# Softmax over 16384 rows: chunks of 17 and 15 rows per partition instead of 16

## Chip, cores, metric

One core of a Trainium2 chip. The metric is the device time of one execution in microseconds (us), lower is better. All runs quoted here were in the fast state. A profile is one execution; its span is 1.8 to 1.9 us shorter than the time measured for it.

## The reference

```python
batch, seq, dim = 16, 1024, 512            # x: float32, random normal
x_max = np.max(x, axis=-1, keepdims=True)
exp_x = np.exp(x - x_max)
return exp_x / np.sum(exp_x, axis=-1, keepdims=True)
```

That is a softmax of 16384 independent rows of 512 values, 2 KB each: 33.55 MB to read and as many to write.

## The kernel before

The rows are cut into ten chunks. A chunk of R rows per partition is 128 x R rows of DRAM; partition p gets R neighbouring rows, so it is one piece of R x 2 KB per partition, and the next partition's piece begins R x 2 KB further on. The second number is the place in an SBUF buffer of 96 rows per partition; chunks 8 and 9 reuse the places of chunks 0 to 3. (The comments are added here.)

```python
CHUNKS = [
    (3, 0), (5, 3), (8, 8), (16, 16), (16, 32), (16, 48), (16, 64), (16, 80), (16, 0), (16, 16),
]
EARLY = 8                            # loads issued at the start, on the SP queue
AFTER_STORE = {2: [8], 3: [9]}       # later loads, once a place is free
GROUP = 8                            # rows computed at a time
STORE_ROWS = {3: 8, 4: 8, 5: 8}      # these chunks are stored in halves, on the ACT queue
ON_VECTOR = 3                        # the last groups are scaled on VectorE
# ... (cut)
    for R, _ in CHUNKS:
        for flat, views in ((x_flat, src), (out_flat, dst)):
            part = flat[at : at + P * R, :]
            views.append(part.rearrange("(p r) d -> p r d", r=R))
        at += P * R
# ... (cut)
    for k, (R, _) in enumerate(CHUNKS):
        m = -(-R // GROUP)
        cuts = [R * i // m for i in range(m + 1)]
```

For each group of rows VectorE takes the maxima, ScalarE does exp with sums, GpSimd scales (VectorE in the last three groups), and ScalarE's queue issues the store.

## Time and profile before

| | before |
|---|---|
| time, six runs | 161.50 us median, 161.43 to 161.58 |
| span of the profile | 159.6 us |
| bytes moved | 67.13 MB in 3315 packets |
| busy share of the most used compute engine (ScalarE) | 58% |

One more view turned out to be needed, and I had not looked at it closely enough: the DMA in the last microseconds. Here it is for the window from 156.0 to 159.4 us, cut into 40 slices of 0.085 us. A packet is counted in the slice in which it begins, and a packet of the last store lasts 1.21 us.

```profile
DMA  8809988800088880800000000000000000000000
q10 hardware_dynamic: 34, 0.59, 40.4%
```

The 16 DMA engines do not begin their last packets together. Most do so in the first eight slices, up to 156.7 us; the last one begins in the 17th slice, at 157.36. It lands 1.21 us later, at 158.57. The execution is over only when that one engine is done.

### The profile page before, as it was taken

The page shows a single profiled execution, that of the slowest core. Times are in us where ns is not written, and L with a number is a line of the kernel's source. Part 1 is how long each engine was busy: PE and PEld are TensorE (multiplying, and loading weights), DVE is VectorE, ACT ScalarE, POOL GpSimd, SP SyncE. Part 2 cuts the span into 40 slices and gives each one's busy share as a digit, 9 for nine tenths or more (in the row PEclk, how much of TensorE's full clock was granted, in tenths as well). Part 3 has the DMA queues.
Part 4 walks back from the last instruction along what each step waited for, and adds up shares of the span by engine and source line. Part 5 has one row for each costly group of instructions (what it writes and reads, how often), then busy time and mean ns, then how long its engine had stood idle before and what let it go on. Part 6 is the DMA issues. An engine that isn't in the chain of part 4 may idle for free.

```text
span 159.6 us, 442 instructions
## 1 busy us (share of the span) xinstructions
DVE 82.6 (52%) x58; ACT 92.9 (58%) x257; POOL 91.2 (57%) x18
## 2 busy tenths in 40 slices
DVE  0470903980966567393856768386479935000000
ACT  0719076039949796976979957993995760000000
POOL 0060912950899999999999999999930000000000
DMA  7999999999999999999999999989999999999994
GB/s 271 439 464 398 431 391 435 458 408 421 431 423 431 427 415 443 411 468 423 431 456 411 437 423 431 464 378 448 406 468 443 445 411 419 476 411 419 468 419 172
DMA packets 3315, 67.13 MB, mean 421 GB/s; under 512 B 368, under 2 KB 368, under 8 KB 624
## 3 DMA queue, kind: packets, MB, share of 16 engines
q1 hardware_dynamic: 1440, 33.56, 49.6%
q10 hardware_dynamic: 1872, 33.56, 49.0%
q14 instruction: 3, 0.02, 0.0%
HBM read 33.55 MB, written 33.55 MB: 420 GB/s over the span
## 4 chain that ended last, share of the span: by engine, by line
POOL 51%; issue 12%; ACT 11%; DVE 7%; DMA 3%; ACTq 0%; DVEq 0%; POOLq 0%
POOL held L150 51%; ACT held L135 11%; DVE held L157 4%; DMA held<-in_x_dram 3%; DVE shift L127 3%; ACTq L163 0%; DVE recip L147 0%; DVEq L209 0%; POOLq L150 0%; DVEq L147 0%; ACTq L135 0%
## 5 line engine op out<-in xcount | busy, mean ns | idle before, releaser
L135 ACT ACTIVATE held<-held,shift 128x512 f32<-128x512 f32 x128 | 90.4, 708 | 33.0 <-POOL held L150 29.9
L150 POOL TENSOR_TENSOR held<-held,recip 128x4096 f32<-128x4096 f32 (+2 forms) x14 | 91.0, 6529 | 25.8 <-DVE recip L147 25.8
L127 DVE TENSOR_REDUCE shift<-held 128x8 f32<-128x4096 f32 (+2 forms) x17 | 70.3, 4139 | 5.4 <-DMA held<-in_x_dram 5.4
L147 DVE RECIPROCAL recip<-sums 128x8 f32<-128x8 f32 (+2 forms) x17 | 3.4, 200 | 45.9 <-ACT held L135 45.9
L135 ACT ACTIVATION_READ_ACCUMULATOR held<-held,shift 128x1 f32 x128 | 24.0, 187 | 0.0
L157 DVE TENSOR_SCALAR held<-held,recip 128x512 f32<-128x512 f32 x24 | 10.0, 491 | 0.1
L135 ACT ACT_TABLE_LOAD x1 | 1.3, 1283 | 4.5 <-DMA held<-in_x_dram 4.5
L198 POOL MEMSET const-float32-0.0<- 128x1 f32 x1 | 0.1, 98 | 0.2 <-issue 0.2
L198 POOL MEMSET const-bfloat16-1.0<- 128x1 bf16 x1 | 0.1, 101 | 0.0
L198 POOL MEMSET const-uint8-127<- 128x1 uint8 x1 | 0.1, 101 | 0.0
L198 POOL MEMSET const-float32-1.0<- 128x1 f32 x1 | 0.1, 98 | 0.0
## 6 DMA issues: line engine op xcount, KB each, us to landing
held<-in_x_dram SPq DMA_DIRECT2D x7, 4096.0 KB, 39.1
out_dram<-held ACTq DMA_DIRECT2D x4, 4096.0 KB, 29.1
out_dram<-held ACTq DMA_DIRECT2D x7, 2048.0 KB, 37.9
held<-in_x_dram SPq DMA_DIRECT2D x1, 2048.0 KB, 11.5
held<-in_x_dram SPq DMA_DIRECT2D x1, 1280.0 KB, 7.1
out_dram<-held ACTq DMA_DIRECT2D x1, 1280.0 KB, 20.5
held<-in_x_dram SPq DMA_DIRECT2D x1, 768.0 KB, 4.4
out_dram<-held ACTq DMA_DIRECT2D x1, 768.0 KB, 15.8
```

The costliest lines, as they stand in the source:

```text
L127: nc.vector.reduce_max(out=shift[g], in_=place[k][:, a:b, :], axis=AX, negate=True)
L135: nc.scalar.activation(out=place[k][:, r, :], in_=place[k][:, r, :], func=EXP, bias=shift[g][:, r - a : r - a + 1], scale=1.0, accum_out=s ...
L147: nc.vector.reciprocal(out=recip, in_=sums[g])
L150: nc.gpsimd.tensor_tensor(out=place[k][:, a:b, :], in0=place[k][:, a:b, :], in1=recip.unsqueeze(2).to_broadcast([P, b - a, d]), op=mybir.A ...
L157: nc.vector.tensor_scalar_mul(out=place[k][:, r, :], in0=place[k][:, r, :], scalar1=recip[:, r - a : r - a + 1],)
L198: nc = _bacc.Bacc("TRN2", target_bir_lowering=False, num_devices=1)
```

## The change

The intent is to use odd numbers of rows, so that the pieces of neighbouring partitions no longer lie a power of two apart in DRAM. Chunk 2 shrinks from 8 to 7 rows and the 16-row chunks become 17 and 15 in turn. The rule for groups is rounded so that 17 rows remain two groups (8 and 9).

```diff
 CHUNKS = [
-    (3, 0), (5, 3), (8, 8), (16, 16), (16, 32), (16, 48), (16, 64), (16, 80), (16, 0), (16, 16),
+    (3, 0), (5, 3), (7, 8), (17, 15), (15, 32), (17, 47), (15, 64), (17, 79), (15, 0), (17, 15),
 ]
-STORE_ROWS = {3: 8, 4: 8, 5: 8}
+STORE_ROWS = {3: 8, 4: 7, 5: 8}
-        m = -(-R // GROUP)
+        m = max(1, round(R / GROUP))
```

## The prediction

> **What bounds the kernel now.** I read the head of the profile page first (busy shares and the 40 slices), then the DMA queues and the list of DMA issues, then the busy time by stretches, then the DMA queues of single stretches, and last the timeline of the end. Head of the page and DMA parts:
>
> ```profile
> DVE 82.6 (52%) x58; ACT 92.9 (58%) x257; POOL 91.2 (57%) x18
> ...
> DMA  7999999999999999999999999989999999999994
> ...
> DMA packets 3315, 67.13 MB, mean 421 GB/s; under 512 B 368, under 2 KB 368, under 8 KB 624
> ...
> q1 hardware_dynamic: 1440, 33.56, 49.6%
> q10 hardware_dynamic: 1872, 33.56, 49.0%
> ...
> held<-in_x_dram SPq DMA_DIRECT2D x7, 4096.0 KB, 39.1
> out_dram<-held ACTq DMA_DIRECT2D x4, 4096.0 KB, 29.1
> ```
>
> No compute engine is over 58% busy, while the 16 DMA engines are 90% busy or more in all slices but the first, one in the middle (8 tenths) and the last. The two queues' packets fill 49.6% + 49.0% = 98.6% of the span: 157.4 of 159.6 us. Loads (q1) and stores (q10) move 33.56 MB each, and nothing can take those bytes away. The 4 MB stores land 29.1 us after issue, though at 430 GB/s one needs 4.19 MB / 430 = 9.8 us: they stand in a queue. So the bound is the transfers' packet time, not a wait of an engine. The chain that ended last (POOL 51%, ACT 11%) follows engines that feed stores into a queue that already has work; I don't take it as the bound.
>
> By stretches (us; instruction counts in brackets; the last two columns are the DMA share and GB/s):
>
> ```profile
> 2.00:12.00 10.00, 4.64 (x3) 3.52 (x8) 2.75 (x1) 1.00 1.05 445
> 12.00:22.00 10.00, 4.48 (x2) 4.77 (x13) 4.46 (x1) 1.00 0.99 405
> 22.00:41.00 19.00, 9.64 (x5) 11.20 (x33) 7.56 (x2) 1.00 1.01 424
> 60.00:80.00 20.00, 13.49 (x6) 16.27 (x46) 20.00 (x4) 1.00 1.00 433
> 109.00:155.00 46.00, 19.30 (x29) 17.13 (x48) 8.21 (x2) 1.00 1.01 435
> ```
>
> Everywhere from 2 to 155 us the DMA is full, at about 430 GB/s. The exception is 12 to 22 us: engines just as busy, but 405 GB/s; 22 to 41 is slightly low at 424. The loads' queue in three stretches (12 to 22, 22 to 41, 76 to 90 us) says whose packets are slow:
>
> ```profile
> q1 hardware_dynamic: 110, 3.60, 88.1%
> ...
> q1 hardware_dynamic: 223, 6.26, 78.3%
> ...
> q1 hardware_dynamic: 142, 4.13, 68.4%
> ```
>
> A share times 16 engines times the stretch is the packets' time: 141.0, 238.0 and 153.2 us, that is 25.5, 26.3 and 27.0 bytes per ns and engine. Against 27.0 the first stretch lost 7.4 and the second 5.8 engine-us, together 13.2, or 13.2 / 16 = 0.83 us of the span. The single packet records agree: a 32 KB load packet has a median of 1213 ns and a mean of 1229 over 896 packets, (1229 - 1213) x 896 / 16 = 0.9 us, nearly all before 41 us.
>
> The end:
>
> ```profile
> 134.00 0.34 ACTq L163 DMA_DIRECT2D out_dram<-held  x1
> ```
>
> The last store is issued at 134.0 and the span ends at 159.6: 25.6 us, against 9.8 for its own transfer. Compute thus has about 15 us of slack before the end.
>
> **What the Trainium skill says.** "DMA: Bandwidth & Descriptors", section "Bandwidth", gives a fabric ceiling of 435 GB/s (16 ports) and a measured 425 for 16 MB on one core. The trace's 433 and 435 in its steady stretches sit there, so no layout can speed these up. The same page, "Queues, rings and completion order", says that each DMA engine goes round robin between its queues, one packet at a time. The trace agrees: from 76 to 90 us loads (32 KB a packet) have 68.4% of the engines' time and stores (16 KB) 33.1%, two to one with nearly equal packet counts (142 and 137). The page's "Latency and other measured facts" says that copies whose rows lie a large power of two apart (2 MiB, 4 MiB) lose up to half of their rate, full rate at 512 KiB, mechanism unverified. The rows of a partition here lie 32 KB apart, far below, and the trace shows them at the ceiling from 41 us on; only the dip of 12 to 41 us could be something alike, with all engines walking near each other. No run shows that yet.
>
> **The change part by part.**
>
> *Packet sizes and number.* Each partition is one packet of R x 2 KB. Packet records: 16 KB takes 611 ns, 32 KB 1213 (10 KB 385, 6 KB 234). So 16 KB costs 602 ns, 27.2 bytes per ns, and each packet about 9 ns on top. A 17-row packet then should take 1213 + 75 = 1288 ns, 15 rows 1138, 7 rows 536, 9 rows 686. Loads stay 10. Stores stay 13: one each for chunks 0 to 2, two each for chunks 3 to 5 (8+9, 7+8, 8+9 rows; before 8+8), one each for the last four. The rounding in the group rule keeps two groups in a chunk of 17 rows. Bytes equal, packets equal (128 x 23 = 2944): the sum of nominal times changes by 0.0 us.
>
> *The slow loads.* This is the only term that an odd pitch can shrink. If odd spacing removes the whole dip, -0.9 us; if it is a matter of reads running with few stores beside them, 0. Packets of 16 KB pitch (chunk 2, at 8 to 12 us, loads alone) ran at 611 to 616, without loss, so reads alone are not slow as such and pitch or chance phase remain. I take half: -0.4 us.
>
> *Compute.* VectorE takes the last three groups: 8 + 8 + 9 = 25 rows instead of 24, one more scaling of 0.49 us; the 9-row reduction is 4.39 x 9/8 = 4.9 us instead of 4.39, the last group has one more exp at about 0.7 us. GpSimd has 103 rows instead of 104, 0.88 us less (7.02 / 8 a row). The last store comes some 1 to 2 us later: all within the 15 us of slack, 0.
>
> *The loads that wait for buffers.* Load 8 goes to rows 0 to 14, which are chunks 0, 1, 2 exactly, as before (0 to 15). Load 9 waits for both stores of chunk 3, whose second is now 9 rows. Up to there the stores carry 3+5+7+8+9 = 32 rows, as before 3+5+8+8+8. Packets alternate, so the second store lands at nearly the same time, within 1 us. Before, load 9 was issued at 85.4 and the load ahead of it landed at 95.1: near 10 us of slack, 0.
>
> *The end.* Each engine still ends with 8 packets of the last store; a packet of 1.29 instead of 1.21 us makes the ragged end at most 0.1 us longer. The start (first chunks of 3 and 5 rows) is untouched.
>
> Sum: 0.0 - 0.4 + 0 + 0 + 0.1 = -0.3 us: 161.46 - 0.3 = about 161.1.
>
> **The rivals.**
>
> 1. The dip disappears and the start gets faster, too: 160.4. For it: the dip is in the large even pitches only. A floor: all packets at nominal 27.0 bytes per ns give 67.13 MB / 16 / 27.0 = 155.4 us, plus 1.9 us until the first load packet, plus about 0.7 of ragged end, plus the 1.9 us by which the measured time exceeds the span (161.46 - 159.6): 159.9. Faster than 158.2 (2%) is out of reach.
>
> 2. Pitch has no part in it; the dip is reads running into one another before stores spread the engines out, and returns for 17 rows as for 16: 161.4 to 161.6.
>
> 3. Packets over 32 KB are cut in two, or are slower. Cut, a 17-row packet costs 9 ns more, 6 DMAs of 17 rows x 128 x 9 / 16 = 0.4 us, and the round robin would give stores more of the engines and loads less, so loads would land later; the 15 us of slack would take most of that. 161.5 to 162.5. Nothing in the profile of before has such a packet, so I can't exclude it.
>
> 4. Compute becomes the bound through 9-row groups. Against it: GpSimd's busiest stretch is full at 20 of 20 us already, but what it feeds is a backlog, and its rows fall by one. I give it under 1%.
>
> **Range and chances.** Predicted 161.1 us. The ends come from rival 1 (160.4) and from rivals 2 and 3 together (161.9). Faster by over 2% needs less than the floor: 1%. Slower by over 2% (above 164.7) needs 3.2 us of new idle time in the DMA engines or packets 2% slower throughout: 2%. Within 2%: 97%.
>
> **What would show it right or wrong.** Right: packets still 3315 within a few, both queues near 98%, 17-row packets near 1288 ns and 15-row ones near 1138, steady stretches at 430 to 435 GB/s, the last store issued some 15 us before it is needed. The stretch from 12 to 22 us decides between rivals 1 and 2: 425 GB/s or more against 405 again. Wrong: a slice in the middle with a DMA share below 8 tenths, a load issued after the one ahead of it has landed, 17-row packets well off 1288, or a packet count up by hundreds (cut packets).

## The result

Changed kernel: 161.91 us median of six runs (161.46 to 162.17). Before, in the same rounds: 161.50 (161.43 to 161.58). The ratio is 1.0023, 95% interval 1.0006 to 1.0039. Ratios here are the mean time of one kernel's fast runs over that of the other's of the same rounds, so not quite the ratio of the medians. It is slightly slower, where I had expected slightly faster, and much less steady: a range of 0.71 us instead of 0.15.

The page of the changed kernel (an execution of 162.14 us, span 160.3):

```profile
DVE 82.7 (52%) x59; ACT 93.0 (58%) x257; POOL 90.5 (56%) x18
...
DMA  7998989999999999999999998999998999999993
...
DMA packets 3315, 67.13 MB, mean 419 GB/s; under 512 B 368, under 2 KB 368, under 8 KB 624
...
q1 hardware_dynamic: 1440, 33.56, 49.5%
q10 hardware_dynamic: 1872, 33.56, 48.7%
```

The compute engines have the same busy times, and packets and bytes are the same. The two queues' shares fell by 0.4 points together because the span grew, not because packets got shorter: 98.2% of 160.3 is 157.4 us, as before.

By stretches:

```profile
2.00:12.00 10.00, 4.64 (x3) 3.60 (x8) 2.75 (x1) 1.00 1.06 446
12.00:22.00 10.00, 3.95 (x2) 4.77 (x13) 4.46 (x1) 1.00 0.99 402
22.00:41.00 19.00, 11.82 (x5) 12.05 (x35) 8.35 (x2) 1.00 1.00 424
60.00:80.00 20.00, 13.60 (x7) 17.26 (x48) 19.49 (x3) 1.00 1.01 437
109.00:155.00 46.00, 19.81 (x30) 17.85 (x50) 8.20 (x2) 1.00 1.00 432
```

The dip from 12 to 22 us is still there: 402 GB/s against 405. The odd distances did nothing for it here. The issue of the last store moved from 134.00 to 136.24 us:

```profile
136.24 0.34 ACTq L163 DMA_DIRECT2D out_dram<-held  x1
```

The 0.7 us shows up in the window from 156.0 to 159.4 us:

```profile
DMA  0009999090099090000900090000000000000000
q10 hardware_dynamic: 34, 0.63, 42.9%
```

Most engines again begin their last packet by slice 9, at 156.8 us at the latest, little later than before. But two packets begin very late, in slices 20 and 24. The last one begins at 157.96 us and lasts 1.29, so it lands at 159.25, against 158.57 before. That is 0.68 us, the whole difference of this profile (162.14 - 161.45 = 0.69).

The trace's packet records also hold the 16 small packets with which the engines report the end of a DMA. From them I take for each run the **spread of the last landings**: the last engine's report for the last store minus the first engine's. Before it was 1.07 us, with the changed kernel 1.65. The median engine reported only 0.07 us later than before.

### The profile page after: what moved, and what is told of

It reads as the page before. It is cut to its first block, busy times and chain, and to the rows that moved or that the text cites. A ratio compares the mean times of both kernels' runs of the same rounds, so it can differ in the third digit from the quotient of the medians.

```text
span 160.3 us, 443 instructions
## 1 busy us (share of the span) xinstructions
DVE 82.7 (52%) x59; ACT 93.0 (58%) x257; POOL 90.5 (56%) x18
## 2 busy tenths in 40 slices
DMA packets 3315, 67.13 MB, mean 419 GB/s; under 512 B 368, under 2 KB 368, under 8 KB 624
## 4 chain that ended last, share of the span: by engine, by line
POOL 52%; ACT 11%; issue 11%; DVE 8%; DMA 3%; ACTq 0%; DVEq 0%; POOLq 0%
POOL held L150 52%; ACT held L135 11%; DVE held L157 4%; DVE shift L127 3%; DMA held<-in_x_dram 3%; ACTq L163 0%; DVE recip L147 0%; DVEq L209 0%; POOLq L150 0%; DVEq L147 0%; ACTq L135 0%
## 5 line engine op out<-in xcount | busy, mean ns | idle before, releaser
L150 POOL TENSOR_TENSOR held<-held,recip 128x4096 f32<-128x4096 f32 (+4 forms) x14 | 90.3, 6470 | 26.4 <-DVE recip L147 26.4
L127 DVE TENSOR_REDUCE shift<-held 128x8 f32<-128x4096 f32 (+4 forms) x17 | 70.3, 4139 | 5.2 <-DMA held<-in_x_dram 5.1
L147 DVE RECIPROCAL recip<-sums 128x8 f32<-128x8 f32 (+4 forms) x17 | 3.4, 203 | 48.2 <-ACT held L135 39.4
```

The source lines that it names most:

```text
L127: nc.vector.reduce_max(out=shift[g], in_=place[k][:, a:b, :], axis=AX, negate=True)
L147: nc.vector.reciprocal(out=recip, in_=sums[g])
L150: nc.gpsimd.tensor_tensor(out=place[k][:, a:b, :], in0=place[k][:, a:b, :], in1=recip.unsqueeze(2).to_broadcast([P, b - a, d]), op=mybir.A ...
```

## The experiments

In all I made twelve runs, each with five rounds (e5: six timings) against the kernel before on the same chip; e1 to e4, e5 to e8 and e9 to e12 ran on three different chips. "Slow load packets" is the time that load packets took beyond the usual time of their size (9 ns plus 27.2 bytes per ns), divided by 16 engines.

| run | ratio (95%) | median, range (us) | profiled run (us) | spread of last landings (us) | time minus spread | slow load packets (us) |
|---|---|---|---|---|---|---|
| before, first profile | | | 161.45 | 1.07 | 160.38 | 1.31 |
| changed, first profile | 1.0023 (1.0006 to 1.0039) | 161.91, 161.46 to 162.17 | 162.14 | 1.65 | 160.49 | 1.46 |
| e1 before again | 0.9998 (0.9985 to 1.0010) | 161.53, 161.46 to 161.60 | 161.46 | 1.09 | 160.37 | 1.20 |
| e2 changed again | 1.0019 (1.0006 to 1.0031) | 161.91, 161.60 to 162.10 | 161.91 | 1.47 | 160.44 | 1.34 |
| e3 16 rows, 115 apart | 0.9981 (0.9968 to 0.9995) | 161.24, 161.21 to 161.33 | 161.21 | 0.89 | 160.32 | 1.20 |
| e4 stores of 7 and 9 | 0.9993 (0.9981 to 1.0006) | 161.43, 161.42 to 161.58 | 161.58 | 1.22 | 160.36 | 1.28 |
| e5 changed, 113 apart | 1.0031 (1.0020 to 1.0042) | 162.05, 161.55 to 162.34 | 161.55 | 1.11 | 160.44 | 1.39 |
| e6 16 rows, 112 apart | 0.9996 (0.9984 to 1.0008) | 161.44, 161.38 to 161.56 | 161.44 | 1.20 | 160.24 | 1.24 |
| e7 16 rows, 128 apart | 0.9990 (0.9978 to 1.0002) | 161.31, 161.22 to 161.47 | 161.22 | 0.90 | 160.32 | 1.31 |
| e8 18 and 14 rows | 1.0032 (1.0019 to 1.0045) | 162.07, 161.93 to 162.21 | 162.21 | 1.77 | 160.44 | 1.52 |
| e9 changed, 128 apart | 0.9998 (0.9986 to 1.0011) | 161.42, 161.35 to 161.57 | 161.41 | 1.07 | 160.34 | 1.45 |
| e10 17 rows throughout | 1.0012 (0.9998 to 1.0026) | 161.65, 161.63 to 161.72 | 161.64 | 1.19 | 160.45 | 1.41 |
| e11 unequal middle | 1.0001 (0.9988 to 1.0013) | 161.48, 161.39 to 161.60 | 161.39 | 1.01 | 160.38 | 1.30 |
| e12 equal middle | 1.0022 (1.0009 to 1.0035) | 161.84, 161.54 to 162.12 | 161.84 | 1.43 | 160.41 | 1.37 |

Two things can be read at once. The time minus the spread is 160.24 to 160.49 us in all 14 profiles: the spread, which ranges from 0.89 to 1.77, carries nearly all of the difference between them. (Time minus spread is the landing of the first engine and a constant: the first engine ends at nearly the same time in every run, and the last one decides.) And the mean of the slow load packets says little: e9 has 1.45 us of them and is as fast as before, e12 has 1.37 and is slower. What goes with the time is how far apart the engines finish.

(The landing times and stretches from packet records in my texts run 0.9 us ahead of the clock of the views, because I set their zero wrongly; differences between two of them, such as spreads, are not touched.)

### e1 and e2: both kernels again

No edit. These are controls, with a second profile of each.

> The kernel before, unchanged, against itself: the control for 5 rounds. Expected ratio 1.000 within 0.001, times 161.4 to 161.6. Its second profile tells how much of the uneven end is fixed: in the first profile of before the landings of the last store on the 16 DMA engines spread over 1.07 us (158.40 to 159.47) and slow load packets cost 0.9 us on average. Theory A (the uneven end is a property of the layout): spread again 1.0 to 1.1 us. Theory B (it is a draw of each execution): spread anywhere from 0.6 to 1.8 us, but then the times of before could not agree within 0.1 us as they did.

> The changed kernel, unchanged: more of its times and a second profile. Expected median 161.8 to 162.0 with a spread of 0.5 us or more between runs, ratio 1.001 to 1.004. In its first profile (162.14 us) the typical DMA engine ended its last store no later than before (median end within 0.1 us) and the slowest was 0.7 us later. If the time is set by the slowest engine, this profile's spread of the last landings will fit its own time: spread of last landings about (time - 160.5) us.

Before: 161.46 to 161.60 and a spread of 1.09 us, as in its first profile. So theory A holds for this layout: the unevenness of before is reproducible. The changed kernel again had a median of 161.91, with 0.50 us between its fastest and slowest run, and this profile has a spread of 1.47 us at 161.91. The rule that I had written down (spread = time - 160.5) gives 1.41.

### e3: only the distance in DRAM, first try

Theories: P, the odd distance of rows makes the changed kernel slower; S, the unequal packet sizes do; and the hope of my prediction, that an odd distance helps. The edit lets several chunks share one region of DRAM, of which each partition owns a run of rows. Sizes, order and compute are those of before. (Softmax goes row by row, so which rows go into which chunk does not alter the result.)

```diff
+REGIONS = [[1], [2], [0, 3, 4, 5, 6, 7, 8, 9]]
# ... (cut: src and dst become lists of fixed length)
-    for R, _ in CHUNKS:
+    for members in REGIONS:
+        R = sum(CHUNKS[k][0] for k in members)
         for flat, views in ((x_flat, src), (out_flat, dst)):
-            part = flat[at : at + P * R, :]
-            views.append(part.rearrange("(p r) d -> p r d", r=R))
+            part = flat[at : at + P * R, :].rearrange("(p r) d -> p r d", r=R)
+            r = 0
+            for k in members:
+                views[k] = part[:, r : r + CHUNKS[k][0], :]
+                r += CHUNKS[k][0]
```

> Only the distance of the rows in DRAM changes: packet sizes, order and compute are those of before (16 rows, stores of 8), but chunks 0 and 3 to 9 are cut out of one region of 115 rows a partition, so that a partition's rows lie an odd 230 KB from the next one's instead of 32 KB. Theory P (the odd distance is what makes the changed kernel slower and less steady): 161.8 to 162.1 and a spread between runs of 0.4 us or more. Theory S (uneven packet sizes do it): 161.4 to 161.6, steady, as before. If an odd distance helps, as my prediction half assumed: 160.6 to 161.1, and 12 to 22 us at 425 GB/s instead of 405.

Measured 161.24 us, ratio 0.9981: theory P is wrong, and this kernel beats the one before by 0.2% and the changed one by 0.4%. It is steady. Its window from 156.0 to 159.4 us:

```profile
DMA  0089998800008800000000000000000000000000
```

The last packet begins in slice 14, at 157.1 us. The list of DMA issues of e3 has this line for the first load:

```profile
held<-in_x_dram SPq DMA_DIRECT2D x1, 768.0 KB, 4.0
```

These 768 KB land 4.0 us after issue. The same list of before has 4.4:

```profile
held<-in_x_dram SPq DMA_DIRECT2D x1, 768.0 KB, 4.4
```

The reports of the engines for the first load tell why. Before, the last three of the 16 came 0.58, 0.81 and 0.90 us after the first, the other 13 within 0.20. In e1 it was 0.56, 0.91 and 0.92, with the changed kernel 0.56, 0.90 and 0.96. In e3 all 16 lay within 0.54, with no group apart. The load did not become faster, only more even: the mean of the 16 reports is 3.46 us after the start of the span, before it is 3.40. The dip from 12 to 22 us shrank in part (416 GB/s instead of 405).

### e4: only the sizes of the stores

```diff
-STORE_ROWS = {3: 8, 4: 8, 5: 8}
+STORE_ROWS = {3: 7, 4: 9, 5: 7}
+CUT = {3: 7, 4: 9, 5: 7}
-        cuts = [R * i // m for i in range(m + 1)]
+        cuts = [0, CUT[k], R] if k in CUT else [R * i // m for i in range(m + 1)]
```

> Only the stores' sizes change: loads of 16 rows as before, but the six stores of chunks 3 to 5 have 7, 9, 9, 7, 7, 9 rows instead of 8. Theory S (packets of unequal size break the regular alternation of a 32 KB load and a 16 KB store, and the engines drift apart): 161.7 to 162.1 and less steady. Theory P (distance of rows): 161.4 to 161.6. If loads alone matter (their size over 32 KB, or the unlike load sizes): 161.4 to 161.6 too.

Measured 161.43 us, ratio 0.9993. The stores of 7 and 9 rows cost nothing measurable. If unequal sizes matter, it is those of the loads.

### e5: the changed sizes, far apart

The changed kernel with `REGIONS = [[0], [1], [2], [3, 4, 5, 6, 7, 8, 9]]`: chunks 3 to 9 are 226 KB apart.

> The changed kernel's sizes, order and stores, but chunks 3 to 9 are cut out of one region of 113 rows a partition, so that the rows of neighbouring partitions lie 226 KB apart instead of 34 or 30 KB; chunks 0 to 2 as in the changed kernel. So far every profile fits time = 160.4 us + the spread of the last store's landings over the 16 engines (before 1.07 and 1.09, changed 1.65 and 1.47, the run with 115 rows 0.89, the run with stores of 7 and 9 rows 1.22). Theory P2 (the extra 0.5 us of the changed kernel is lost by two engines on loads whose neighbours lie 30 or 34 KB apart): 161.3 to 161.5, spread at most 1.1 us. Theory S2 (the sizes of 17 and 15 rows themselves do it): 161.8 to 162.0, spread 1.4 us or more.

Measured 162.05 us, ratio 1.0031, from 161.55 to 162.34. Theory P2 is wrong: the cost stays when the distance is changed. The profile fell on the fastest of the six runs (161.55) with a spread of 1.11 us, so it fits the relation of time and spread but does not show what a slow run looks like.

### e6 and e7: where the gain of e3 came from

The kernel before with `REGIONS = [[0], [1], [2], [3, 4, 5, 6, 7, 8, 9]]` (112 rows, 224 KB apart) and with `REGIONS = [list(range(10))]` (all ten chunks, 128 rows, 256 KB apart).

> The kernel before with chunks 3 to 9 in one region of 112 rows a partition (224 KB apart, an even number), chunks 0 to 2 untouched. Together with the run with 115 rows, where chunk 0 was in the region too, it tells whether its gain of 0.3 us came from the start or from the later loads. If from the later loads being far apart: 161.1 to 161.3 and slow load packets from 12 to 23 us at most 0.3 us on average. If the odd number matters: 161.5 and 0.5 us. If the start of chunk 0 gave it all: 161.4 to 161.6, with two engines some 0.7 us late already where chunk 2 lands.

> The kernel before with all ten chunks in one region of 128 rows a partition: rows of neighbouring partitions 256 KB apart, a power of two. If powers of two collide: slow load packets well over the 1.3 us of before and 162 us or more. If only being far apart matters: as with 115 rows, 161.1 to 161.3, first chunk landed by 4.65 us instead of 4.95.

With 112 rows the time was that of before (161.44, ratio 0.9996), and the late engines were there again: 0.56, 0.86 and 0.89 us at the first load. With 128 rows all engines reported the first load within 0.33 us, and the time was 161.31; its ratio of 0.9990 has an interval that just includes 1. So the gain goes with chunk 0: it lies far apart in e3 and e7 and contiguous in e6. The times alone would not decide this, as the three intervals overlap; the reports of the first load and the spreads (0.89 and 0.90 against 1.20 us) do. An odd number plays no part: 128 did not collide, 113 did not help.

### e8: even numbers in the form of the change

```diff
+    (3, 0), (5, 3), (6, 8), (18, 14), (14, 32), (18, 46), (14, 64), (18, 78), (14, 0), (18, 14),
+STORE_ROWS = {3: 9, 4: 7, 5: 9}
```

> The changed kernel's form with even numbers: loads of 3, 5, 6 and then 18 and 14 rows in turn, stores of 9 and 7. Neighbours lie 36 and 28 KB apart. If odd numbers are what costs: 161.4 to 161.6. If unequal loads, or loads over 32 KB with neighbours near each other, cost: 161.8 to 162.1, as in the changed kernel, with a spread of the last landings of 1.4 us or more.

Measured 162.07 us, ratio 1.0032, spread 1.77. The same form with even numbers costs as much, so oddness is not the cause. Here, too, two packets begin late in the window of 156.0 to 159.4 us, in slices 22 and 23:

```profile
DMA  0090999990000909000009900000000000000000
```

### e9: the changed kernel without the late engines

`REGIONS = [list(range(10))]` on the changed kernel. In e5 chunks 0 to 2 were left contiguous; here they lie 256 KB apart as well.

> The changed kernel with all ten chunks, the first three too, cut out of one region of 128 rows a partition. With 115 or 128 rows the loads of the first chunks were even: no engine was late where chunk 2 landed (spread 0.33 to 0.54 us instead of 0.8), and the time fell to 161.2 to 161.3; with 113 rows and the first chunks left alone the changed kernel stayed at 162.05. Theory L (what costs is that engines which are late from the start lose more on loads of unequal size): without late engines nothing is amplified, 161.2 to 161.5, spread of the last landings at most 1.1 us. Theory S3 (unequal load sizes cost by themselves): 161.7 to 162.0.

Measured 161.42 us, ratio 0.9998, and steady again (161.35 to 161.57). The engines reported the first load within 0.38 us. Its window from 156.0 to 159.4 us:

```profile
DMA  0099999900090990000000000000000000000000
```

The last packet begins in slice 15, at 157.2 us, and the stragglers at 157.6 and later are gone. This is the outcome that theory L named: the changed sizes cost 0.3 to 0.5 us only where some engines are late from the first load on. Two reservations. The 16-row kernel in the same layout (e7) had 161.31 us, so some 0.1 us may remain as the cost of the sizes; that is within the noise. And e9 moves chunks 0, 1 and 2 at once, so it does not show that it is chunk 0's place, and not that of the 7-row chunk 2, that matters for the changed sizes. It differs from e5 also in 128 against 113 rows for the later chunks, but neither distance made a difference of this size for the 16-row kernel (e6, e7).

The dip is gone in e9: 431 GB/s from 12 to 22 us. Yet the slow load packets still sum to 1.45 us. Those that begin from 12 to 23 us fell from 0.56 us (changed kernel) to 0.07, while those of the first load rose from 0.26 to 0.76. So the dip was not time that a layout had only to win back; here the slow packets moved to another place.

### e10: seven chunks of 17 rows

```diff
+    (3, 0), (6, 3), (17, 9), (17, 26), (17, 43), (17, 60), (17, 77), (17, 0), (17, 17),
+EARLY = 7
+AFTER_STORE = {2: [7], 3: [8]}
+STORE_ROWS = {2: 8, 3: 8, 4: 8}
```

> Loads of 3, 6 and then seven times 17 rows (nine loads, twelve stores, the buffers moved accordingly): over 32 KB a packet, odd, but all alike. If packets over 32 KB or odd numbers cost: 161.7 to 162.1, unsteady. If it is the alternation of unlike sizes that costs: 161.3 to 161.6 and steady within 0.25 us. The 17-row load begins at 9 us instead of 12, which may make the early losses somewhat larger.

Measured 161.65 us, ratio 1.0012 with an interval that includes 1, and very steady (0.09 us between runs). It lies between the two theories. All I take from it is that packets over 32 KB are not by themselves what makes the time unsteady.

### e11 and e12: the change cut into two halves

The first has the changed sizes in chunks 4 to 7 only, the second everywhere but there. Both have the changed rounding of groups.

```diff
e11:
+    (3, 0), (5, 3), (8, 8), (16, 16), (15, 32), (17, 47), (15, 64), (17, 79), (16, 0), (16, 16),
+STORE_ROWS = {3: 8, 4: 7, 5: 8}
e12:
+    (3, 0), (5, 3), (7, 8), (17, 15), (16, 32), (16, 48), (16, 64), (16, 80), (15, 0), (17, 15),
```

> Half of the change: chunks 0 to 3 and the last two as before (3, 5, 8, 16 and 16, 16), chunks 4 to 7 of 15, 17, 15, 17 rows with the stores of the changed kernel. The slow load packets all lie before 50 us, which are chunks 3, 4 and 5. If the unlike sizes of chunks 4 to 7 cost: 161.7 to 162.1. If the cost is in chunks 2 and 3 (7 rows, then 17): 161.4 to 161.6.

> The other half: 3, 5, 7, 17, then 16, 16, 16, 16, and 15 and 17 at the end, stores of chunk 3 8 and 9 rows, the others 8. If the cost is in chunks 2 and 3: 161.7 to 162.1 and unsteady. If it is in the unlike sizes of chunks 4 to 7: 161.4 to 161.6 and steady. Both halves at 161.7 would mean that each break in the sizes adds its part.

This splits the change cleanly. With only the middle unequal: 161.48 us, ratio 1.0001, steady. With the middle equal and the rest changed: 161.84, ratio 1.0022, from 161.54 to 162.12, which is the changed kernel's behaviour. The windows from 156.0 to 159.4 us, first of e11, then of e12:

```profile
DMA  0809909008080908000000000000000000000000
```

```profile
DMA  0999990900990090900900000000000000000000
```

In e11 the last packet begins in slice 16 (157.28 us), one before that of the kernel before; in e12 in slice 20 (157.6). (The expectation of e11 says that all slow load packets lie before 50 us, in chunks 3 to 5. That isn't quite so: the first load, chunk 0, has 0.26 us of them in the changed kernel, and 0.10 us lie after 50 us.) What e12 shares with the changed kernel and e11 doesn't is chunk 2 of 7 and chunk 3 of 17 rows (and the 15 and 17 at the end, whose loads come after the stretch in which load packets are slow). That the last two play no part is argued, not tested, and whether it is the 7 or the 17 that matters I did not separate.

## Why the prediction was right or wrong

The measured 161.91 us lies on the upper end of the predicted range (160.4 to 161.9), and "within 2%" was right. But the sign of the small effect was wrong, and that the time still fell on the end of the range was luck: I had put that end there for slow loads that stay (rival 2) and cut packets (rival 3), and what moved the time from rival 2's 161.5 to there was in neither.

- **The bound: right.** DMA packets fill the span before and after; bytes and packets did not change. Packet times came out as computed: a median of 1288 ns for 17 rows, 1138 for 15, 686 for 9, 535 for 7 (computed 536). Packets over 32 KB are not cut (3315 packets), so rival 3 is out.
- **The slow loads, -0.4 us: wrong.** They did not shrink: 402 against 405 GB/s from 12 to 22 us, slow load packets 1.46 and 1.34 us against 1.31 and 1.20 before. By my own test this excluded rival 1 and spoke for rival 2. The distance of rows has an effect, but in the first chunks, and the change leaves chunks 0 and 1 as they were. Nor was the dip time to be won: in e9 it is gone, and the slow load packets sum to the same 1.45 us.
- **Compute and waits for buffers, 0: right.** The last store was issued 2.2 us later (I had said 1 to 2). It still has to queue behind other stores, and the end did not follow it.
- **The end, at most 0.1 us: this is the term that failed.** I had taken the ragged end for the grain of one packet. It is the lateness of the slowest of 16 engines, whose last packets no other engine took over, though the first one had ended 1.07 us earlier. It grew by 0.58 us in the first profile of the changed kernel and by about 0.4 in the second. With the hoped-for -0.4 us absent too, that makes the result.
- **Rival 2 (161.4 to 161.6)** rightly said that the dip would stay, and lacked the growth of the end; its own reason for the dip was not tested. Rival 4 found nothing to support it.
- Slips: my texts give 85.4 us for the issue of load 9 and 95.1 for the landing before it; by the clock of the views it is 84.5 and about 94.2, with the same distance. And in my floor the first load packet begins 1.0 us after the start of the span, not 1.9, and another 1.0 us passes between the last landing and the end of the span, which I had left out. These two nearly cancel.

What the runs show, in order. Chunk 0 lies contiguous in DRAM, and its load leaves three engines 0.5 to 1.0 us late (seen in all eleven profiles with that layout, in none of the three with chunk 0 far apart). With the sizes of the change in chunks 2, 3, 8 and 9 the spread at the end is 1.43 to 1.65 us in three of four profiles, and 1.11 in the fourth (e5). With the first chunks far apart the same sizes cost nothing that can be measured (e9). Why these sizes add to the lateness stays open.

The reports of the later DMAs, which I had not used, show how the lateness is carried. Once the loads are done only stores run, and the spread hardly changes any more: in the kernel before it is 1.07 us for the store that lands at 109 us and 1.07 for the last, in the changed kernel 1.68 and 1.65. So the end is nearly settled by 109 us. In the first store that lands after the last load, the third-latest engine reports 0.62 to 0.89 us after the median one in all eleven profiles with chunk 0 contiguous, and 0.14 to 0.19 in the other three. So three engines are late by then just where the first load left three late. That they are the same ones is still an inference: the packet records carry no engine number, and where I linked packets by their times the chains were not unique.

In e3 and e7 one engine is late by then all the same, 0.75 and 0.72 us after the median, and the first load is hardly its cause: the spread is 0.39 and 0.40 for the load that lands at 79 us, and 0.90 and 0.91 for the next load. The page of e3 has a third queue:

```profile
q14 instruction: 3, 0.02, 0.0%
```

One of these three packets begins at 88.1 us and takes 309 ns, and a load packet that begins 0.3 us later takes 286 ns longer than usual (252 in e7). If both are on one engine, that is 0.6 us, a little more than the spread grew by. After the third of them, at 126.1 us, a second engine of e3 is late (0.65 us after the median instead of 0.24). All 14 profiles have three such packets. That they set the 0.9 us that is left in e3 and e7 is likely, but no run tests it.

## What to carry to other kernels

When DMA is full from start to end, look at when each DMA engine finishes, not only at how full they are on average: the time is that of the slowest engine, and it can move by half a microsecond with bytes, packets and the sum of packet times unchanged. Look for the cause at the first load already. Here laying chunk 0 out so that neighbouring partitions read far apart was worth 0.2% (e3, the best version found), while changing the sizes of loads in a pattern that runs steadily was a risk with little to gain.

## What the Trainium skill lacked or had wrong

- "DMA: Bandwidth & Descriptors" says that engines 7 and 15 are usually slower than the others (section "Latency and other measured facts"), which the records here, without engine numbers, can't show. It has no figure for how far apart the 16 engines finish; here the last landings are 0.89 to 1.77 us apart, and the time less this spread is 160.24 to 160.49 us in all profiles.
- The same page, section "Latency and other measured facts", warns of rows a large power of two apart, with marked losses from 2 MiB on; that no loss was seen at 256 KB (e7, 161.31 us against 161.50) agrees with it. What it lacks is that a contiguous layout, which it names as a cure, can be the uneven one: the reports of the first load lie within 0.33 and 0.38 us at 256 KB and 0.54 at 230 KB, against 0.89 to 1.00 when contiguous.
- No page that I read says whether a packet of 34 KB is cut: here none was (3315 packets as before), and its 1288 ns follow the same line (9 ns plus 27.2 bytes per ns) as the 611 ns of 16 KB.
